# A hybrid decoder layer on one core: w_o split a head earlier and one tile per head, a new deal of the filling products, squares written to an operand block

## The chip, the core and the metric

The kernel runs on one core of one Trainium2 chip. The metric is the device time of one execution, in microseconds (us). Three runs of the kernel before gave 1396.53 to 1400.5 us, median 1399.54 us. Engine names in the profile: PE is TensorE (PEld its weight loads), DVE VectorE, ACT ScalarE, POOL GpSimd, SP the engine that issues the transfers.

## The reference

One decoder layer over 1024 tokens of width 1024, all in float32. Four retention heads and eight causal attention heads (latent attention, key width 96, value width 64) share one input projection; their outputs, 512 columns each, are joined and multiplied by one output matrix w_o. Two normalisations stand around the residual, then a SwiGLU with 2816 hidden columns and a gated embedding:

```python
def rmsnorm(x, w):
    xf = x.astype(jnp.float32)
    y = xf * lax.rsqrt(jnp.mean(xf * xf, axis=-1, keepdims=True) + EPS)
    return (y * w.astype(jnp.float32)).astype(x.dtype)
...
    return jnp.concatenate([ret_out, mla_out], axis=-1) @ w_o
...
        h = h + rmsnorm(mix, post_mix_norm[i])
        hn = rmsnorm(h, pre_ffn_norm[i])
        ff = (jax.nn.silu(hn @ w_gate[i]) * (hn @ w_up[i])) @ w_down[i]
        h = h + rmsnorm(ff, post_ffn_norm[i])
        e = rmsnorm(p[i] @ w_ple_proj[i], ple_norm[i])
        gate = jax.nn.sigmoid(h @ w_ple_gate[i] + b_ple_gate[i])
        h = h + e * gate
```

## The kernel before

Every float32 operand of a large product is split into a high and a low part: ACT casts the high part (line 81), DVE or POOL subtracts it for the low one (line 82). A product is then three matmuls, high by high, low by high and high by low (line 94). The splits of whole weight tiles are made by `slot` (line 102 issues the load of a tile `raw`, four buffers; the parts go into a ring of eight high/low slots, or into a place that is handed in as `hl`).

The order of each engine's own queue is set by a scheduler from the program's order, the waits and its own estimates of times; only the steady gate/up stage at the end has an order that is written out by hand. Buffers come from pools with a fixed count; PSUM has the tags s (two buffers of two banks), t, f and o.

The stages, with their places in the profiled execution:

- The input projection, the latent projections and the four retention heads, up to about 350 us. The retention outputs are stored to `md`.
- Sixteen products of p with w_pp, half of a row tile each, stored to `ed`; they run beside attention heads 0 and 1.
- The attention heads, `for h in range(NH)`, to about 564 us. Each head loads its k and q operands (`heads(h)`, lines 536 and 537, eight loads). For each of eight row blocks i there is a score product `sc` (PE, line 94), the masked minimum (DVE, line 612), the exponential (ACT, line 617), the reciprocal (DVE, line 620) and the scaling (POOL, line 621). Then pairs of blocks are transposed (`ptp`, PE, line 630), split into th and tl (ACT and DVE) and multiplied by the values (`po`, lines 641 and 642). Each half of a head ends with `os` (ACT and DVE, lines 647 and 648) and four stores to `mo` (line 650).
- Between them the filling products: the retention half of the output projection. `product_to` (lines 545 to 555) is a generator: each `advance` by one (line 557) makes one half row tile, 12 matmuls named `fill`, copied out by DVE (line 554) and stored to `od` once two are there. Sixteen are dealt: 2 after a head's first half and 1 after its second in heads 2 to 5, one after the first half in heads 6 and 7, the rest behind the last head (line 655). Their operands: `mr`, the four retention outputs (line 581; split into bh and bl, by ACT and POOL), and the first four tiles of w_o (`wo`, line 584, split by ACT and DVE), both at the head of `h == 2`. The other four tiles of w_o (`wo2`, line 652) are loaded and split at the end of head 4, into the upper halves of bh and bl.
- The output projection, `project(n)` for eight row tiles. It splits the attention output (`mh` by ACT, `ml` by POOL, two buffers each), multiplies it by wo2 into a PSUM tile `po3` of two banks (24 matmuls), and DVE adds the filling products' part out of PSUM into `mix` (line 715). ACT squares `mix` for the norm (line 717), POOL raises the mean to −1/2 (line 113), DVE scales (719) and adds the residual (720), SP stores (721), ACT squares again (723), DVE multiplies by the next norm's weights (725) and ACT scales (726). Both squares write their unused result into the same PSUM tile, so the tile is free for the next but one row tile only after line 723. `operands(n)` then transposes the rows into the operand blocks `xt` (PE, line 686, `ptx`; for the later four tiles POOL first makes the four subtractions of lines 739 to 742).
- The gate/up products `gu` (line 834) over the operand blocks, with weights loaded into `graw` and one of the `duo` tiles, summed by POOL, split, and used as `gh` and `gl`; the steady part, from 681 us, keeps PE busy without a gap. Then the down projection, the gate and the end.

The lines of the change: 584 and 587 (`wo`), 652 (`wo2`), 644 (the deal), 717 and 723 (the squares), 777 (`graw`) and 889 (`load(0)`).

Of the kernel before, what the change touches and what calls it, by code (L numbers as in the profile page):

```python
# [11 lines left out]
F32 = mybir.dt.float32  # L12
# [8 lines left out]
P = 128  # L21
# [41 lines left out]
def hybrid_layer(ctx: ExitStack, tc: tile.TileContext, a: dict, out: bass.AP):  # L63
# [508 lines left out]
    pe_ = scoped(st3, "pe", side="right")  # L572
    pm = scoped(st2, "pm", 2)
    vb = None

    for h in range(NH):
        kh_, kl_, qh, ql = heads(h) if h else first
        if h == 2:
            for k in range(RH):
                raw = raws.tile([P, S], F32, tag="raw", name=f"mr{k}")  # L580
                sp.dma_start(out=raw, in_=md[k])
                for c in range(2):
                    cs = slice(c * 512, (c + 1) * 512)
                    split(*bx(k, cs), raw[:, cs], sub=pool)
            wo = [slot(a["w_o"][k], name=f"o{k}") for k in range(4)]
            gen = product_to(od, [bx(k, slice(0, S)) for k in range(4)], wo, dve.tensor_copy)
            next(gen)
        if h == 1:
            vb = pm.tile([P, NT, 2 * VD], F32R, name="vb", bufs=1)
        vt = va if h % 2 == 0 else vb  # L590
        sp.dma_start(out=vt.bitcast(F32), in_=vd[h])
        for gg in range(2):
            cs = slice(gg * 512, (gg + 1) * 512)
            po = ps1("po", "of"[gg] if h >= 3 else "o")
            for g in (2 * gg, 2 * gg + 1):
                pb = []
                sc = ps2("sc") if g < 2 else None
                for i in (2 * g, 2 * g + 1):
                    n = (i + 1) * P
                    c1 = slice(i * P, (i + 1) * P)  # L600
                    if g >= 2:
                        sc = ps2("sc")
                    o = (i % 2) * 512 if g < 2 else 0
                    nc_ = 1 if n <= 512 else 2
                    w = max(n // nc_, 256)
                    for c in range(nc_):
                        products(sc[:, o + c * 512 : o + c * 512 + w],
                                 [(qh[:, c1], ql[:, c1], kh_[:, c * w : (c + 1) * w], kl_[:, c * w : (c + 1) * w])])
                    w = n // nc_
                    sv = sc[:, o : o + nc_ * 512].rearrange("p (c n) -> p c n", c=nc_)[:, :, :w]  # L610
                    nm = small.tile([P, 1], F32, name="nm")
                    dve.tensor_tensor_reduce(  # L612
                        out=sv, in0=sv, in1=cmask[:, S - n :].rearrange("p (c n) -> p c n", c=nc_),
                        scale=-1.0, scalar=3.0e38, op0=ALU.add, op1=ALU.min, accum_out=nm)
                    pr_ = pm.tile([P, S], F32, name="pr", bufs=5)
                    rs = small.tile([P, 1], F32, name="rs")
                    act.activation(pr_[:, :n].rearrange("p (c n) -> p c n", c=nc_), sv, AF.Exp, bias=nm, scale=-1.0,  # L617
                                   accum_out=rs)
                    ri = small.tile([P, 1], F32, name="ri")
                    dve.reciprocal(out=ri, in_=rs)  # L620
                    pool.tensor_tensor(out=pr_[:, :n], in0=pr_[:, :n], in1=ri.broadcast_to([P, n]), op=ALU.mult)  # L621
                    pb.append(pr_)
                last = 2 * g + 1
                for jj in range(g + 1):
                    blk = [(2 * jj, 0), (2 * jj, 1), (2 * jj + 1, 0), (2 * jj + 1, 1)]
                    if jj == g:
                        blk = [blk[0], blk[1], blk[3]]
                    pt = ps1("ptp")
                    for m, (kk, qq) in enumerate(blk):
                        pe.transpose(pt[:, m * P : (m + 1) * P], pb[qq][:, kk * P : (kk + 1) * P], ident)  # L630
                    nn = len(blk) * P
                    th = pm.tile([P, 512], F32R, name="th", bufs=4)[:, :nn]
                    tl = pm.tile([P, 512], F32R, name="tl", bufs=4)[:, :nn]
                    split(th, tl, pt[:, :nn])
                    off = (g % 2) * 256
                    for kk in (2 * jj, 2 * jj + 1):
                        if kk < last:
                            src, dst = slice((kk % 2) * 256, (kk % 2) * 256 + 256), slice(off, off + 256)
                        else:
                            src, dst = slice(256, 384), slice(off + 128, off + 256)  # L640
                        pe.matmul(po[:, dst], vt[:, kk, :], th[:, src], start=(kk == 0), stop=False)  # L641
                        pe.matmul(po[:, dst], vt[:, kk, :], tl[:, src], start=False, stop=(kk == last))  # L642
            if h >= 2:
                advance(gen, "fo"[gg], (2, 1)[gg] if h < 6 else 1 - gg)
            os_ = pm.tile([P, 512], F32, name="os")
            rows = slice((h % 2) * 64, (h % 2) * 64 + 64)
            act.copy(out=os_[rows], in_=po[64:])
            dve.tensor_tensor(out=os_[rows], in0=po[:64], in1=os_[rows], op=ALU.add)
            for i in range(4):
                sp.dma_start(out=mo[4 * gg + i][rows, h // 2, :], in_=os_[rows, i * P : (i + 1) * P])  # L650
        if h == 4:
            wo2 = [slot(a["w_o"][4 + k], name=f"o{4 + k}", hl=(bh[1][:, k, :], bl[1][:, k, :])) for k in range(4)]

    act.activation(small.tile([P, 1], F32, name="warm", bufs=1), rs, AF.Silu)
    advance(gen, "f", 2 * NT)
# [49 lines left out]
    def project(n):  # L705
# [6 lines left out]
        for c in range(2):  # L712
            cs = slice(c * 512, (c + 1) * 512)
            products(pt[:, cs], [(mh[:, k, :], ml[:, k, :], wo2[k][0][:, cs], wo2[k][1][:, cs]) for k in range(4)])
        dve.tensor_tensor(out=mix, in0=pt, in1=mix, op=ALU.add)
        ss = small.tile([P, 1], F32, name="s3")
        act.activation(pt, mix, AF.Square, accum_out=ss)
        rsqrt(ss, ss, 1.0 / D)
        dve.scalar_tensor_tensor(out=mix, in0=mix, scalar=ss, in1=wpm, op0=ALU.mult, op1=ALU.mult)
        dve.tensor_tensor(out=ht, in0=ht, in1=mix, op=ALU.add)  # L720
        sp.dma_start(out=hd[t], in_=ht)
        ss = small.tile([P, 1], F32, name="s3")
        act.activation(pt, ht, AF.Square, accum_out=ss)  # L723
        rsqrt(ss, ss, 1.0 / D)
        dve.tensor_tensor(out=mix, in0=ht, in1=wpf, op=ALU.mult)
        act.activation(mix, mix, AF.Copy, scale=ss)
# [29 lines left out]
    for n in range(NT):  # L756
        if n == 7:
            load_tiles(7)
        project(n)
        if n % 4 < 2:  # L760
            load_rows(n + (4 if n < 4 else 2))
        if n >= 2:
            operands(n - 2)
        if n < 4:
            load_tiles(n + 3)
    st_m.close()
    st_b.close()

# [5 lines left out]
    ghl = [[pg_.tile([P, 2, HALF], F32R, name=f"g{n}{i}") for n in "hl"] for i in (1, 2, 3, 0)]  # L774
    ghl = ghl[3:] + ghl[:3]
    quad = [v.rearrange("p (i n) -> p i n", i=4) for v in duo]
    graw = [pg_.tile([P, 4, HALF], F32, name="graw"), quad[0]]
    gga = [quad[2], quad[3]]
    gs = [v.rearrange("p (i n) -> p i n", i=3) for v in (strip[:, : 3 * HALF], strip[:, 3 * HALF :])] + [quad[4][:, :3]]
    wd = quad[4]  # L780
# [6 lines left out]
    def load(m):  # L787
        name, q = mats[m]
        sp.dma_start(out=graw[m % 2], in_=a[name][q])
# [96 lines left out]
    def when(i, f, *args):  # L886
        todo[i].append((f, args))

    load(0)
    load(1)  # L890
    weight_part(0, 0)
    weight_part(1, 0)
# [275 lines left out]
```

## Time and profile before

| | |
|---|---|
| median of three runs | 1399.54 us (1396.53 to 1400.5) |
| profiled execution | 1400.68 us |
| its span, first to last instruction | 1398.9 us |
| mean granted clock of TensorE | 0.986 |
| PE busy | 1336.5 us, 96% |
| DVE busy | 770.9 us, 55% |
| ACT busy | 541.8 us, 39% |
| POOL busy | 461.8 us, 33% |
| moved by transfers | 214.73 MB, 153 GB/s |

The span is taken from the first instruction to the last, so the execution's own time is a little longer (1.8 us here). Matmuls are pipelined, so a row of 0.39 us stands for a matmul that begins 0.23 us after the one before. In a row of the timeline, what stands in brackets is how long the engine was idle ahead of the row, and what ended that.

### The profile page before, as it was taken

Reading aid. Unit: us, or ns where it says so; the run is one execution under the profiler, and the core shown is the slowest. Engines: PE = TensorE matmul, PEld = TensorE weight load, DVE = VectorE, ACT = ScalarE, POOL = GpSimd, SP = SyncE. Lnnn points to the kernel's source line nnn. Section 1 sums busy time; section 2 is a strip of 40 time slices with the busy share of each in tenths; the row PEclk is TensorE's granted clock in tenths of the full one; section 3 lists DMA queues with packets and bytes.
Section 4 is the critical chain, followed back from the end, with each engine's and each line's share of the span. In section 5 each row is a group of like instructions: output and inputs, shape, how many; then the busy total and the mean of one; then the engine's idle time right before and its main releaser. Section 6 shows DMA issues by size and latency. Waiting matters only on the chain.

```text
span 1398.9 us, 18091 instructions
## 1 busy us (share of the span) xinstructions
PE 1336.5 (96%) x6756; PEld 1134.4 (81%) x6756; DVE 770.9 (55%) x1193; ACT 541.8 (39%) x898; POOL 461.8 (33%) x341
## 2 busy tenths in 40 slices
PE   7999999999989999887999999999999999999997
PEld 6987988988778887665788888888888788888886
DVE  6445637445566676488445444444445554474645
ACT  5443321011565555355343333333334444344521
POOL 1100000000363333248577666666664100012500
PEclk9999999999999999998999999999999999999999
DMA  7127831212474641743344344433346876565422
GB/s 251 46 92 250 265 118 39 75 23 60 143 232 123 200 131 30 273 135 123 121 165 149 146 173 173 169 138 144 140 178 218 269 234 211 178 218 193 138 102 75
DMA packets 85304, 214.73 MB, mean 153 GB/s; under 512 B 8992, under 2 KB 23840, under 8 KB 79584
## 3 DMA queue, kind: packets, MB, share of 16 engines
q1 hardware_dynamic: 85216, 213.58, 45.5%
q8 instruction: 53, 0.87, 0.3%
q14 instruction: 35, 0.29, 0.1%
HBM read 144.86 MB, written 67.63 MB: 152 GB/s over the span
## 4 chain that ended last, share of the span: by engine, by line
PE 83%; DMA 4%; DVE 4%; POOL 3%; issue 3%; ACT 2%; SPq 1%; DVEq 0%; ACTq 0%; POOLq 0%
PE gu L834 29%; PE db L1011 7%; PE pqk L94 6%; PE pg L94 6%; PE da L1011 6%; PE pa L94 4%; PE fill L94 3%; PE prv L94 3%; PE sc L94 3%; PE ptp L630 2%; PE prg L94 2%; PE pge L94 2%; PE po L642 1%; PE pq L94 1%; PE po L641 1%
## 5 line engine op out<-in xcount | busy, mean ns | idle before, releaser
L834 PE MATMUL gu<-x,gh 128*128 128x512 f32 x1232 | 383.6, 393 | 6.3 <-ACT po L723 5.6
L834 PEld LDWEIGHTS gu<-x,gh 128*128 128x128 f32 x1232 | 233.2, 190 | 55.7 <-ACT po L723 5.8
L834 PE MATMUL gu<-x,gl 128*128 128x512 f32 x616 | 241.2, 392 | 0.4 <-DVE gl L82 0.4
L834 PEld LDWEIGHTS gu<-x,gl 128*128 128x128 f32 x616 | 116.7, 189 | 25.1 <-DVE gl L82 0.7
L845 ACT COPY duo<-gu 128x512 f32<-128x512 f32 x66 | 38.9, 589 | 189.3 <-PE gu L834 189.3
L621 POOL TENSOR_TENSOR pr<-pr,ri 128x128 f32<-128x128 f32 (+3 forms) x64 | 74.8, 1178 | 105.7 <-DVE ri L620 98.4
L113 POOL TENSOR_TENSOR s<-s,mhalf 128x1 f32<-128x1 f32 x32 | 23.9, 752 | 238.4 <-DVE s L111 238.3
L113 POOL TENSOR_TENSOR gf<-gf,mhalf 128x4 f32<-128x4 f32 x8 | 8.1, 1008 | 266.7 <-DVE gf L111 266.7
L82 DVE TENSOR_TENSOR gl<-strip,gh 128x1024 fp32r<-128x1024 f32 (+1 forms) x44 | 61.6, 1399 | 33.3 <-ACT gh L81 33.3
L82 DVE TENSOR_TENSOR x<-draw,x 128x1024 fp32r<-128x1024 f32 (+1 forms) x43 | 48.1, 1135 | 46.9 <-ACT x L81 46.9
L82 DVE TENSOR_TENSOR gl<-graw,gh 128x1024 fp32r<-128x1024 f32 x22 | 33.8, 1538 | 72.5 <-ACT gh L81 72.5
L81 ACT CAST x<-draw 128x1024 fp32r<-128x1024 f32 (+1 forms) x47 | 45.2, 979 | 73.0 <-PE db L1011 20.6
L82 DVE TENSOR_TENSOR gl<-duo,gh 128x1024 fp32r<-128x1024 f32 x22 | 29.5, 1343 | 67.9 <-ACT gh L81 67.9
L850 DVE TENSOR_TENSOR duo<-gu,duo 128x512 f32<-128x512 f32 x66 | 45.4, 687 | 38.0 <-PE gu L834 37.9
L82 DVE TENSOR_TENSOR tl<-ptp,th 128x512 fp32r<-128x512 f32 (+1 forms) x80 | 49.8, 633 | 24.7 <-ACT th L81 23.7
L94 PE MATMUL pg<-x,x 128*128 128x512 f32 (+1 forms) x255 | 58.9, 378 | 0.0
L81 ACT CAST th<-ptp 128x512 fp32r<-128x512 f32 (+1 forms) x80 | 42.4, 544 | 41.9 <-PE ptp L630 41.6
L855 POOL TENSOR_TENSOR duo<-duo 128x512 f32<-128x512 f32 x11 | 23.3, 2122 | 103.2 <-DVE duo L818 103.2
L617 ACT ACTIVATE pr<-sc,nm 128x128 f32<-128x128 f32 (+3 forms) x64 | 47.7, 747 | 18.7 <-DVE nm L612 11.1
L94 PEld LDWEIGHTS pg<-x,x 128*128 128x128 f32 x255 | 45.8, 188 | 8.6
L612 DVE CUSTOM_DVE_ANT_0 sc<-sc,cmask 128x128 f32<-128x128 f32 (+3 forms) x64 | 48.0, 770 | 7.7 <-PE sc L94 7.3
L94 PE MATMUL pqk<-bl,hi_r 128*128 128x512 f32 x128 | 50.7, 396 | 0.0
(368 smaller groups left out, 3418.5 us busy)
## 6 DMA issues: line engine op xcount, KB each, us to landing
draw<-ld SPq DMA_DIRECT2D x58, 256.0 KB, 3.8
graw<-in_w_gate SPq DMA_DIRECT2D x11, 1024.0 KB, 8.6
duo<-in_w_up SPq DMA_DIRECT2D x11, 1024.0 KB, 4.7
duo<-in_w_down SPq DMA_DIRECT2D x11, 1024.0 KB, 5.1
td<-duo SPq DMA_DIRECT2D x11, 1024.0 KB, 4.4
ld<-duo SPq DMA_DIRECT2D x11, 1024.0 KB, 4.4
draw<-td SPq DMA_DIRECT2D x36, 256.0 KB, 4.1
ld<-duo SPq DMA_DIRECT2D x11, 768.0 KB, 6.7
```

Of the source, the lines that this page charges most:

```text
L81: act.copy(out=hi, in_=src)
L82: sub.tensor_tensor(out=lo, in0=src, in1=hi.bitcast(F32), op=ALU.subtract)
L94: pe.matmul(dst, l, r, start=(m == 0), stop=(m == n - 1))
L113: pool.tensor_tensor(out=dst, in0=dst, in1=mhalf[:, :n], op=ALU.pow)
L612: dve.tensor_tensor_reduce(out=sv, in0=sv, in1=cmask[:, S - n :].rearrange("p (c n) -> p c n", c=nc_), scale=-1.0, scalar=3.0e38, op0=ALU. ...
L617: act.activation(pr_[:, :n].rearrange("p (c n) -> p c n", c=nc_), sv, AF.Exp, bias=nm, scale=-1.0, accum_out=rs)
L621: pool.tensor_tensor(out=pr_[:, :n], in0=pr_[:, :n], in1=ri.broadcast_to([P, n]), op=ALU.mult)
L630: pe.transpose(pt[:, m * P : (m + 1) * P], pb[qq][:, kk * P : (kk + 1) * P], ident)
L834: pe.matmul(dst, l[:, at, ks], r[:, k, :], start=(n in (0, 1, 3) and x == 0), stop=(x == 11), skip_group_check=True)
L845: act.copy(out=s[nm], in_=dst)
L850: dve.tensor_tensor(out=s[nm], in0=dst, in1=s[nm], op=ALU.add)
L1011: pe.matmul(banks[j], l[:, ls], r[:, rs_], start=(fresh and q == 0 and m == 0), stop=(q == NQ - 1 and m == 2), skip_group_check=True)
```

## The change

- `wo` is made in the block of `h == 1` instead of `h == 2`: its four loads and splits come a head earlier in the program and take four of the eight ring slots there.
- `wo2` is made one tile at a time, at the end of heads 3, 4, 5 and 6, instead of four at the end of head 4.
- The filling products follow a table `FILL`, by head from 2 to 7 and half, and three are made inside the last head, ahead of its last products with the values.
- Both squares of `project` write into `junk`, a quarter of one operand block in SBUF (T4, of which that quarter is written only by the last row tile), seen as eight blocks of 128 columns, instead of into PSUM.
- The first load of w_gate is issued before the pools of the output projection are closed, into `duo[0]`; `graw` and `duo[0]` change places for w_gate and w_up in the whole steady stage.

```diff
+    wo2 = []
+
+    FILL = (0, 1), (2, 1), (1, 1), (1, 1), (1, 1), (0, 0)
...
-            wo = [slot(a["w_o"][k], name=f"o{k}") for k in range(4)]
             gen = product_to(od, [bx(k, slice(0, S)) for k in range(4)], wo, dve.tensor_copy)
             next(gen)
         if h == 1:
+            wo = [slot(a["w_o"][k], name=f"o{k}") for k in range(4)]
...
                     off = (g % 2) * 256
+                    if h == NH - 1 and g == 3 and jj < 3:
+                        advance(gen, "o", 1)
...
             if h >= 2:
-                advance(gen, "fo"[gg], (2, 1)[gg] if h < 6 else 1 - gg)
+                advance(gen, "fo"[gg], FILL[h - 2][gg])
...
-        if h == 4:
-            wo2 = [slot(a["w_o"][4 + k], name=f"o{4 + k}", hl=(bh[1][:, k, :], bl[1][:, k, :])) for k in range(4)]
+        if 2 < h < 7:
+            k = h - 3
+            wo2.append(slot(a["w_o"][4 + k], name=f"o{4 + k}", hl=(bh[1][:, k, :], bl[1][:, k, :])))
...
+        junk = xt[6][:, :, :, 3 * P :].rearrange("p h k n -> p (h k) n")
         ss = small.tile([P, 1], F32, name="s3")
-        act.activation(pt, mix, AF.Square, accum_out=ss)
+        act.activation(junk, mix.rearrange("p (b n) -> p b n", b=8), AF.Square, accum_out=ss)
...
-        act.activation(pt, ht, AF.Square, accum_out=ss)
+        act.activation(junk, ht.rearrange("p (b n) -> p b n", b=8), AF.Square, accum_out=ss)
...
+    sp.dma_start(out=duo[0].rearrange("p (i n) -> p i n", i=4), in_=a["w_gate"][0])
     st_m.close()
...
-    graw = [pg_.tile([P, 4, HALF], F32, name="graw"), quad[0]]
+    graw = [quad[0], pg_.tile([P, 4, HALF], F32, name="graw")]
...
-    load(0)
     load(1)
```

What this does to the engines' orders is seen in three places. First SP, in the loads and stores of heads 1 and 2. The order before, from the third `ed` store ahead of the retention loads on:

```order
L555 DMA ed_100<-fill 128x1024
L581 DMA mr_3859<-md 128x1024
L581 DMA mr_3865<-md 128x1024
L581 DMA mr_3871<-md 128x1024
L591 DMA va<-vd 128x1024
L650 DMA mo_114<-os 64x128
...
L555 DMA ed_101<-fill 128x1024
L581 DMA mr_3877<-md 128x1024
L102 DMA raw_o_3883<-in_w_o 128x1024
L102 DMA raw_o_3889<-in_w_o 128x1024
L650 DMA mo_110<-os 64x128
```

The changed order at the same place:

```order
L555 DMA ed_100<-fill 128x1024
L102 DMA raw_o_3597<-in_w_o 128x1024
L102 DMA raw_o_3603<-in_w_o 128x1024
L102 DMA raw_o_3609<-in_w_o 128x1024
L594 DMA va<-vd 128x1024
...
L102 DMA raw_o_3615<-in_w_o 128x1024
L555 DMA ed_101<-fill 128x1024
L584 DMA mr_3883<-md 128x1024
L536 DMA hi_k_3871<-kd_76 64x1024
L537 DMA hi_k_3871<-krd_82 32x1024
...
L537 DMA lo_q_3878<-qrd_81 32x1024
L584 DMA mr_3889<-md 128x1024
```

The w_o tiles stand where three retention loads stood. Head 2's k and q loads, which before stood in the rows ahead of all of this, now come behind them, and three retention loads last of all.

Second ACT, at the start of the output projection (`mh` is the high part of the attention output; `s` the sum of a square). Before:

```order
L81 CAST mh<-strip 128x512 x2
L717 ACTIVATE po_5763,s_5789<-duo_5741 128x1024
L81 CAST mh<-duo_5740 128x512
L723 ACTIVATE po_5763,s_5796<-duo_5742 128x1024
L717 ACTIVATE po_5809,s_5835<-duo_5738 128x1024
L81 CAST mh<-duo_5740 128x512
L726 ACTIVATE duo_5741<-duo_5741,s_5796 128x1024
```

Changed:

```order
L81 CAST mh<-strip 128x512 x2
L81 CAST mh<-duo_5740 128x512 x2
L81 CAST mh<-strip 128x512
L724 ACTIVATE x_5734,s_5789<-duo_5741 128x8x128
L81 CAST mh<-strip 128x512
L730 ACTIVATE x_5734,s_5796<-duo_5742 128x8x128
L724 ACTIVATE x_5734,s_5835<-duo_5738 128x8x128
L733 ACTIVATE duo_5741<-duo_5741,s_5796 128x1024
```

The squares write the operand block `x` instead of `po`, and the first of them stands behind five `mh` casts instead of two.

Third SP, at the first weight loads of the gate/up stage. Before:

```order
L721 DMA hd_91<-duo_5742 128x1024
L789 DMA graw<-in_w_gate 128x2048
L702 DMA duo_5741<-od_109 128x1024
L789 DMA duo_5738<-in_w_up 128x2048
L721 DMA hd_93<-duo_5742 128x1024
```

Changed:

```order
L797 DMA graw<-in_w_up 128x2048
L728 DMA hd_92<-duo_5742 128x1024
...
L728 DMA hd_91<-duo_5742 128x1024
L773 DMA duo_5738<-in_w_gate 128x2048
L728 DMA hd_93<-duo_5742 128x1024
```

w_up comes first now, four row tiles' stores earlier; w_gate stands behind the seventh row tile's store as before, but it writes a `duo` block that the transposes of an earlier row tile must have left.

## Rows read from the trace of the kernel before

**Rows 1.** The page's part 4: the chain that ended last, share of the span by engine.

```profile
PE 83%; DMA 4%; DVE 4%; POOL 3%; issue 3%; ACT 2%; SPq 1%; DVEq 0%; ACTq 0%; POOLq 0%
```

**Rows 2.** Stretches: length, busy PE, PEld, DVE, ACT, POOL (instructions), PEclk, DMA, GB/s.

```profile
399.80:428.90 29.10, 24.32 (x134) 20.23 (x134) 22.16 (x44) 20.22 (x41) 22.05 (x18) 0.94 0.73 207
428.90:450.40 21.50, 21.17 (x138) 19.09 (x137) 13.84 (x34) 10.91 (x26) 6.78 (x7) 1.00 0.48 119
...
472.60:499.60 27.00, 23.86 (x148) 21.16 (x146) 19.74 (x45) 15.96 (x32) 9.96 (x8) 1.00 0.64 189
499.60:526.50 26.90, 26.60 (x161) 23.81 (x162) 17.95 (x44) 14.23 (x32) 10.98 (x10) 1.00 0.46 135
...
546.40:571.90 25.50, 21.03 (x93) 16.74 (x92) 8.73 (x14) 8.66 (x15) 3.75 (x3) 0.80 0.23 70
571.90:680.60 108.70, 85.33 (x377) 67.46 (x376) 76.81 (x82) 51.53 (x82) 63.26 (x51) 0.89 0.48 170
...
655.90:662.70 6.80, 4.47 (x11) 3.51 (x12) 6.72 (x7) 3.20 (x5) 6.76 (x4) 0.50 0.19 77
...
681.00:1080.00 399.00, 399.00 (x1762) 330.41 (x1761) 189.32 (x192) 136.85 (x195) 251.24 (x162) 1.00 0.45 164
...
659.14:680.60 21.46, 18.01 (x67) 13.61 (x67) 10.28 (x11) 7.49 (x11) 15.91 (x12) 0.76 0.14 49
...
571.90:591.70 19.80, 17.59 (x81) 14.19 (x79) 11.31 (x12) 6.38 (x10) 6.38 (x7) 1.00 1.01 379
```

**Rows 3.** Timeline of PE, end of head 1 and head 2: waits.

```profile
403.31 0.38 PE L642 MATMUL po<-tl,vb 128*128 128x256 f32 x1 [0.36 <-DVE tl L82]
...
414.82 0.50 PE L94 MATMUL fill<-lo_o,bh 128*128 128x512 f32 x1 [1.34 <-DVE lo_o L82]
```

**Rows 4.** Timeline of PE, stretch from 472.6 us: its two longest waits.

```profile
493.11 0.38 PE L642 MATMUL po<-tl,va 128*128 128x256 f32 x1 [1.75 <-DVE tl L82]
498.00 0.55 PE L630 MATMUL ptp<-pack,pr 128*128 128x128 f32 x3 [0.98 <-POOL pr L621]
```

**Rows 5.** Who waited for instructions on po, 571.9 to 681 us (us, times).

```profile
  PE po L94: 9.2, 6
...
  PE gu L834: 5.6, 1
```

**Rows 6.** Timeline of SP's queue, the retention loads.

```profile
392.57 4.50 SPq L581 DMA_DIRECT2D mr<-md  x3
```

**Rows 7.** Timeline of POOL: retention splits; first subtraction of the last row tile.

```profile
404.25 5.00 POOL L82 TENSOR_TENSOR bl<-mr,bh 128x512 fp32r<-128x512 f32 x4
...
665.99 1.76 POOL L739 TENSOR_TENSOR duo<-duo 128x512 f32<-128x512 f32 x1 [0.44 <-ACT duo L726]
```

**Rows 8.** The chain of waits in order of time: start, us, what.

```profile
425.87 2.74 PE fill L94 x12
...
491.09 3.26 DMA raw_o<-in_w_o
...
565.41 1.90 DMA mo<-os
```

**Rows 9.** Timeline of DVE: a fill copy, an addition alone and beside POOL.

```profile
572.11 0.69 DVE L554 COPY fill<-fill 128x512 f32<-128x512 f32 x1 [3.09 <-PE fill L94]
...
582.64 1.22 DVE L720 TENSOR_TENSOR duo<-duo,duo 128x1024 f32<-128x1024 f32 x1
...
588.70 2.20 DVE L720 TENSOR_TENSOR duo<-duo,duo 128x1024 f32<-128x1024 f32 x1
```

**Rows 10.** Timeline of ACT: the first square, a cast, an activation into SBUF.

```profile
579.32 1.03 ACT L717 ACTIVATE po<-duo 128x1024 f32<-128x1024 f32 x1 [7.80 <-DVE duo L715]
...
582.91 0.62 ACT L81 CAST mh<-duo 128x512 fp32r<-128x512 f32 x1 [2.45 <-DMA duo<-mo]
...
664.76 1.15 ACT L726 ACTIVATE duo<-duo,s 128x1024 f32<-128x1024 f32 x1
```

**Rows 11.** The page's part 6: w_gate's loads, KB each, us to landing.

```profile
graw<-in_w_gate SPq DMA_DIRECT2D x11, 1024.0 KB, 8.6
```

## The prediction

> **What bounds the kernel now.** I began with the chain of waits that ended last: TensorE holds 83% of it, every other engine or transfer 4% or less [rows 1]. So the time goes down only where TensorE idles, runs at its lower clock, or issues less. I then cut the part that the change touches into stretches [rows 2], each from one head's last score product to the next head's. The steady gate/up stage from 681 us has PE busy for 399.0 of 399.0 us and the change leaves its work alone, so whatever moves its start moves the end by as much: the predicted difference is the shift of that start, now 680.6 us. The loss ahead of it lies in three places. Beside heads 1 and 2 PE is busy 24.3 of 29.1 us; in the last head 21.0 of 25.5 us at a mean clock of 0.80; in the output projection 85.3 of 108.7 us at 0.89. Last I read what ended PE's idle time: splits of w_o in the first place [rows 3] and in the stretch from 472.6 us [rows 4], the second square in the output projection [rows 5].
>
> **The change, part by part**
>
> *A. The w_o splits a head earlier, stretch 399.8 to 428.9 us.* Now PE waits 1.34 us for lo_o, and four times for tl behind the same splits on DVE, 0.36 us the first time [rows 3]. In the changed order w_o's splits fall in 398 to 408 us, where the mr loads stood, and the mr splits move behind, to 407 to 426 us. What is queued behind: on SP, seven of head 2's eight k/q loads now stand behind the raw_o loads and one of mr, and the eighth behind four stores of head 1; three mr loads, waiting for buffers, took 4.50 us to issue [rows 6]. Head 2's operands land near 414 us, where they were there long before. On POOL four bl splits take 5.00 us [rows 7], and head 2's normalisations queue behind them. Replaying the two orders with these durations I get the next boundary 0.5 us later: the lo_o wait goes and a wait for head 2's operands comes. Bounds: all these waits go (−3), or head 2 waits one more issue block of 4.50 us (+5).
>
> *B. 428.9 to 546.4 us, five stretches, 117.5 us.* By the order these hold 8 filling products where 12 stood (2, 2, 3, 4, 1 before; 0, 2, 3, 1, 2 now; the stretch ahead keeps 2). One is 12 matmuls and 2.74 us [rows 8], so 4 × 2.74 = 11.0 us of PE work go. Late next is the softmax chain on VectorE: the first stretch has 13.84 us of DVE work with two fill copies, of 0.69 us each [rows 2, 9], beside 21.5 us of span. So a stretch without fills still takes about 19.0 us (I take 2.5 of the 5.5 us that its two fills cost). The second is unchanged at 22.2. The third keeps its three fills and loses what a w_o tile does there, a wait of 1.75 us for tl and 0.98 for pr [rows 4] behind a load of which 3.26 us stand in the chain [rows 8]: 27.0 becomes 24.6. The fourth loses three fills, 8.2 us, of which I take 6.4: 20.5. The fifth gains one, and 19.9 becomes 22.2. Together 108.5 us, −9.0. Bounds: only the waits go (−3), or all the fill time and 2 us of waits do (−13).
>
> *C. Last head, 546.4 to 571.9 us.* Three fills go between head 7's transposes, three stand at the end instead of two. PE idles 4.5 us here at clock 0.80 [rows 2], so three fills, 8.2 us of work, find 4.5 us of idle time and a part of the half-clock time: +1.6 us, between −2 (they also keep the clock up) and +4 (8.2 less the idle time). Those at the end are covered by head 7's last stores and the load back, which hold the output projection until 571.9 us (the last store alone has 1.90 us in the chain [rows 8]); without that cover each would cost its 2.74 us.
>
> *D. Output projection, 571.9 to 680.6 us.* The squares no longer write the PSUM bank, so the next tile's products wait for the DVE addition instead of the second square. That wait is 9.2 us of PE in six and 5.6 us in one ahead of the first gate/up product [rows 5], 14.8 us in all, with half-clock stretches behind (6.8 us at 0.50 [rows 2]). But the order shows what takes its place. ACT now casts five mh ahead of the first square, where it cast two. There are two mh buffers, so the fifth waits until PE has finished tile 2: 571.9 + 72 × 0.228 + 2.74 + 0.62 = 591.7 us (0.228 is 2.74/12, 0.62 the cast), against 579.3 us [rows 10]. The first square is 12.4 us later, and all norms behind it. DVE is what must catch up: of its 76.8 us in this stage 10.3 lie behind the last norm step, at 659.1 us, and 0.7 is a fill copy [rows 2, 9]; three additions of 1.22 us, 3.7, come ahead of the square. That leaves 62.1 us, so the last norm step ends at 653.8 us if DVE never idles. Now it idles 67.4 − 55.2 = 12.2 us between 591.7 and 659.1 (its 76.8 less 11.3 and 10.3 [rows 2]); if it keeps all of that, the step ends at 666.0. The replay, row by row, gives 659.7 to 664.3; I take 662.1: +3. The tail behind it (normalise, four POOL subtractions of which the first takes 1.76 us [rows 7], transposes, splits) stays as long, so the steady stage starts 3 us later though PE itself waits less. w_gate's load, 1 MB and 8.6 us [rows 11], now waits for the operands of the sixth tile, whose block it takes; the first gate/up product waits for it although w_up's 24 stand behind. Issued near 650 us, it is landed and split near 662, beside the last norm step, and adds nothing unless that slips. Bounds of D: −9 and +12 (the rivals).
>
> *The squares themselves.* Sixteen ACT operations write SBUF instead of PSUM: 1.03 us into PSUM, 1.15 for an SBUF-to-SBUF activation of the same size [rows 10], so at most 16 × 0.12 = 1.9 us of ACT, hidden, since ACT is busy 51.5 of 108.7 us [rows 2]. The Trainium skill, "ScalarE: Activation LUTs", section "Step-by-step: what each stage is for", speaks against this edit: PSUM is ScalarE's faster destination, which helps only if TensorE doesn't need most of PSUM. By the bare rule the sum would be up to 1.9 us worse; its caveat holds here.
>
> *The rest.* The swap of the raw weight tiles renames buffers and gives the steady stage the same work: 0, from −1 to +1.
>
> **Sum.** 0.5 − 9.0 + 1.6 + 3.0 = −3.9 us. The profiled execution took 1400.68 us, so 1396.8; the median of the runs, 1399.54, is 1.1 lower, so I forecast **1396 us**, 0.25% less. About 0.3% (4.2 us) is what a measurement of this kernel can tell from no change.
>
> **The rivals**
>
> *R1, slower: the late first square isn't caught up.* DVE keeps its 12.2 us of idle time (+6.9), and five more of its norm passes run beside POOL: the same addition takes 1.22 us alone and 2.20 beside POOL's ml split [rows 9], so +5. D is +12 and the time 1399.5 − 6.9 + 12 = 1405 us. It decides once D exceeds the 6.9 us of A to C. For it: each norm is a chain over ACT, DVE and POOL. Against it: tiles overlap, and many passes are slow already. The Trainium skill, "GPSIMD Engine Reference", section "8. Key points", has GpSimd share its SBUF interfaces with VectorE, in contention when there are two SBUF inputs; the pair of durations agrees.
>
> *R2, much faster: the freed banks pay.* DVE never idles (653.8, −5.3), and half of one half-clock stretch of 6.8 us goes too (−3.4): D is −9, the time 1399.5 − 6.9 − 9 = 1384 us. Against it: nothing in a norm's chain is quicker than before.
>
> *R3, no change: the heads don't get shorter.* If the softmax chain sets each head's length, the fills removed were filling idle time and B is −3: 0.5 − 3 + 1.6 + 3 = +2, so 1402 us. For it: from 472.6 to 499.6 PE idles 3.1 us in spite of three fills. Against it: in B's first and fourth stretch PE is busy all but 0.3 us [rows 2].
>
> That the change doesn't do what it says is a small matter: the table deals none to head 2's first half, yet the order still puts two products ahead of its last scores; B counts by the order.
>
> **How the numbers follow.** Forecast 0.45, R1 0.20, R2 0.17, R3 0.18. The forecast lies at the 0.3% bound (1395.3 us): half of it counts as faster, half as same. R2 is faster, R3 same (0.145) or slower (0.035), R1 slower (0.175) or same. Faster 0.40, same 0.39, slower 0.21. The range, 1384 to 1408 us, takes in R1 with 3 us to spare, R3, and the slower half of R2.
>
> **What would show it.** Right: no PE wait on the second square, the first square near 20 us behind the stage's first product, the five stretches near 108 us, the steady stage from about 677 us. Wrong: the five stretches still over 114 us (R3); a steady start beyond 685 us with most DVE additions at 2.2 us (R1) or before 668 us (R2); head 2's first scores waiting over 5 us for hi_q or lo_q.

## The result and the profile after

The changed kernel took 1410.10 us (median of four runs, 1406.58 to 1410.98) against 1399.38 us: a ratio of 1.0080, interval 1.0058 to 1.0102. Repeated later beside other kernels it took 1412.72 us against 1396.83, ratio 1.0109 (1.0086 to 1.0132). It is slower by about 1%, and above the end of the range at 1408 us. In one run of those below, no_squares, one execution of twelve fell out (1512.24 us at a granted clock of 0.84); its time and ratio are those of the other eleven.

The stretches of the changed kernel, cut at the same events as [rows 2] (length; busy PE, PEld, DVE, ACT, POOL with instructions; granted clock; DMA share; GB/s):

```profile
399.50:431.30 31.80, 24.85 (x134) 20.40 (x134) 20.81 (x42) 20.61 (x42) 20.55 (x17) 0.89 0.87 244
...
450.20:475.50 25.30, 22.07 (x143) 19.67 (x142) 17.57 (x41) 13.91 (x30) 9.12 (x8) 1.00 0.55 161
475.50:501.90 26.40, 24.25 (x151) 21.49 (x150) 18.13 (x45) 15.38 (x33) 11.14 (x10) 1.00 0.50 145
...
542.90:570.70 27.80, 24.83 (x130) 20.41 (x129) 11.71 (x22) 9.76 (x18) 5.84 (x4) 0.94 0.22 63
570.70:685.20 114.50, 88.99 (x389) 70.75 (x389) 75.66 (x83) 52.02 (x83) 63.08 (x50) 0.81 0.47 167
...
590.50:661.80 71.30, 48.47 (x213) 38.40 (x212) 59.38 (x67) 40.74 (x67) 40.48 (x34) 0.72 0.43 144
```

The stretch of heads 1 and 2 (A) takes 31.8 us (29.1 before), the five stretches of B 111.6 (117.5), the last head (C) 27.8 (25.5), the output projection (D) 114.5 (108.7). The steady stage starts at 685.2 us instead of 680.6, and what lies behind that start takes 719.6 us instead of 718.3. This profiled execution, 1406.58 us, was the shortest of its four; that of before, 1400.68 us, was longer than each of the four timed beside it.

The wait that the squares were to remove is gone: where [rows 5] had 9.2 and 5.6 us behind the second square, nothing waits for it, and the gate/up products have 0.7 us of idle time left, for another reason (page, part 5):

```profile
L842 PE MATMUL gu<-x,gh 128*128 128x512 f32 x1232 | 382.3, 392 | 0.7 <-ACT x L81 0.7
```

What came in its place is the prediction's late first square. ACT's timeline at the start of the output projection:

```profile
582.13 0.62 ACT L81 CAST mh<-duo 128x512 fp32r<-128x512 f32 x1 [9.22 <-DMA duo<-mo]
...
589.99 0.62 ACT L81 CAST mh<-strip 128x512 fp32r<-128x512 f32 x1 [3.99 <-PE po L94]
590.52 1.06 ACT L724 ACTIVATE x<-duo 128x1024 fp32r<-128x1024 f32 x1
```

In this stage three casts stand ahead of the square, two that wait for transfers (9.22 and 2.62 us) and a third that waits 3.99 us for PE; the square starts 19.8 us behind the stage's first product, where it started 7.4 us behind. PE, no longer held by the banks, finishes its products early and then has nothing but transposes to wait for (timeline of PE, its longest waits there):

```profile
624.12 1.97 PE L692 MATMUL ptx<-pack,duo 128*128 128x128 f32 x8 [4.10 <-ACT duo L733]
633.90 1.11 PE L692 MATMUL ptx<-pack,duo 128*128 128x128 f32 x4 [7.82 <-ACT duo L733]
```

The stretch around them, columns as above:

```profile
622.00:663.00 41.00, 20.14 (x73) 14.83 (x74) 34.67 (x38) 23.74 (x38) 31.41 (x22) 0.50 0.41 142
```

Its granted clock is 0.50 for 41 us, that is 1.2 GHz instead of 2.4. So the waits for the square did not turn into time: they were exchanged for waits for the norms.

### The profile page after: what moved, and what is told of

The parts are those of the page before. It is cut to its first block, busy times and chain, and to the rows that moved or that the text cites. A ratio compares the mean times of both kernels' runs of the same rounds, so it can differ in the third digit from the quotient of the medians.

```text
span 1404.8 us, 18079 instructions
## 1 busy us (share of the span) xinstructions
PE 1335.7 (95%) x6756; PEld 1134.3 (81%) x6756; DVE 769.5 (55%) x1193; ACT 543.0 (39%) x898; POOL 460.1 (33%) x341
## 4 chain that ended last, share of the span: by engine, by line
PE 84%; DMA 3%; POOL 3%; issue 3%; DVE 3%; ACT 2%; SPq 1%; DVEq 0%; ACTq 0%; POOLq 0%
PE gu L842 29%; PE db L1018 8%; PE pqk L94 6%; PE pg L94 6%; PE da L1018 6%; PE pa L94 4%; PE prv L94 3%; PE fill L94 3%; PE po L94 3%; PE sc L94 3%; PE prg L94 2%; PE pge L94 2%; PE ptp L633 1%; PE pq L94 1%; PE po L647 1%
## 5 line engine op out<-in xcount | busy, mean ns | idle before, releaser
L81 ACT CAST x<-draw 128x1024 fp32r<-128x1024 f32 (+1 forms) x47 | 45.3, 980 | 71.5 <-PE da L1018 20.5
L82 DVE TENSOR_TENSOR gl<-duo,gh 128x1024 fp32r<-128x1024 f32 x22 | 33.7, 1533 | 70.2 <-ACT gh L81 70.2
L82 DVE TENSOR_TENSOR gl<-graw,gh 128x1024 fp32r<-128x1024 f32 x22 | 30.5, 1386 | 67.9 <-ACT gh L81 67.9
```

The lines of the kernel that those rows point to most:

```text
L81: act.copy(out=hi, in_=src)
L82: sub.tensor_tensor(out=lo, in0=src, in1=hi.bitcast(F32), op=ALU.subtract)
```

## The experiments

Lengths in us of the stages A to D in each run's profiled execution, by the same events; "square" is the first square's start behind the stage's first product; ratios are against the kernel before, timed beside each.

| run | ratio (95% interval) | A | B | C | D | square |
|---|---|---|---|---|---|---|
| before | 1 | 29.1 | 117.5 | 25.5 | 108.7 | 7.4 |
| the change | 1.0080 (1.0058 to 1.0102) | 31.8 | 111.6 | 27.8 | 114.5 | 19.8 |
| whole_again | 1.0109 (1.0086 to 1.0132) | 32.3 | 118.7 | 27.4 | 115.5 | 20.6 |
| squares_only | 1.0011 (0.9994 to 1.0029) | 28.8 | 117.9 | 23.6 | 106.2 | 10.3 |
| heads_only | 1.0023 (1.0008 to 1.0037) | 32.9 | 113.1 | 28.1 | 106.9 | 9.7 |
| gate_only | 0.9993 (0.9978 to 1.0008) | 26.6 | 117.9 | 22.6 | 106.7 | 8.0 |
| no_squares | 1.0030 (1.0011 to 1.0048) | 32.8 | 113.2 | 28.1 | 106.1 | 9.7 |
| four_in_tail | 1.0012 (0.9995 to 1.0030) | 32.0 | 116.1 | 28.9 | 105.1 | 11.9 |
| wo_back | 1.0047 (1.0029 to 1.0064) | 29.9 | 110.3 | 27.2 | 115.6 | 20.6 |
| wo_back_four_in_tail | 0.9972 (0.9952 to 0.9992) | 29.7 | 110.9 | 28.9 | 103.8 | 11.8 |
| old_deal | 1.0072 (1.0044 to 1.0099) | 33.5 | 122.1 | 27.0 | 107.1 | 13.8 |
| three_at_end | 0.9966 (0.9949 to 0.9983) | 31.9 | 114.8 | 22.6 | 105.4 | 9.8 |
| squares_three_at_end | 1.0027 (1.0013 to 1.0042) | 26.0 | 115.1 | 22.7 | 116.6 | 19.6 |
| wo_only | 0.9987 (0.9973 to 1.0002) | 34.5 | 119.3 | 22.7 | 102.6 | 7.4 |
| wo_first_in_two | 0.9979 (0.9961 to 0.9996) | 26.6 | 113.5 | 28.9 | 105.8 | 12.1 |
| wo2_only | 1.0031 (1.0013 to 1.0049) | 30.0 | 123.0 | 22.5 | 107.2 | 8.0 |
| fill_only | 0.9984 (0.9971 to 0.9997) | 28.0 | 111.7 | 28.1 | 106.3 | 9.7 |

**1. Three parts alone, and the change without its squares.** Theory S was that the squares cost, by pulling casts ahead on ACT; theory G that w_gate's later load does; theory H that the heads do.

squares_only, on the kernel before:

```diff
-        act.activation(pt, mix, AF.Square, accum_out=ss)
+        act.activation(junk, mix.rearrange("p (b n) -> p b n", b=8), AF.Square, accum_out=ss)
...
-        act.activation(pt, ht, AF.Square, accum_out=ss)
+        act.activation(junk, ht.rearrange("p (b n) -> p b n", b=8), AF.Square, accum_out=ss)
```

> The kernel before with nothing but both squares moved into the operand block. The order of ACT in the output projection then has one mh cast (of the third row tile) between the first addition and the first square, where the whole change has three. Theory S (the squares are what costs: once PE no longer waits for them, mh casts come ahead of the first square on ACT, the norms start late, PE runs out of work behind the products and falls to its lower clock): 3 to 8 us slower than before, 1402 to 1407 us, the output projection 112 to 116 us instead of 108.7. Theory G (the squares pay as such, what costs is w_gate's load behind an operand block): faster by 3 to 9 us, 1390 to 1396 us, no wait of PE on the second square.

Neither: 1397.77 us against 1397.18, no difference that can be told. Both theories fall in this form.

heads_only is the sum of wo_only, wo2_only and fill_only, whose diffs stand below:

> The kernel before with the three edits on the heads alone: w_o a head earlier, one tile of w_o per head, the new deal of the fills. Theory S: the heads behave as in the whole change (the output projection starts 1 us earlier) and the output projection as before, so 1397 to 1400 us, no change that a measurement can tell. Theory H (the edits on the heads lose more than their profile shows, by the clock of the stage behind them): slower by 3 us or more, 1402 us and above.

1400.10 us, 0.2% slower: at the upper end of S's band (1397 to 1400), under H's 1402, and unlike S had it, a difference that can just be told.

gate_only, on the kernel before:

```diff
+    sp.dma_start(out=duo[0].rearrange("p (i n) -> p i n", i=4), in_=a["w_gate"][0])
     st_m.close()
...
-    graw = [pg_.tile([P, 4, HALF], F32, name="graw"), quad[0]]
+    graw = [quad[0], pg_.tile([P, 4, HALF], F32, name="graw")]
...
-    load(0)
```

> The kernel before with nothing but the first w_gate load moved and the two raw weight tiles exchanged. Theory S: within 2 us of before, 1398 to 1402 us. Theory G: 4 to 6 us slower, 1403 to 1406 us, because the first gate/up product waits for w_gate's splits and the steady stage starts at 684 to 687 us.

1396.44 us, no difference. Theory G falls.

no_squares, on the changed kernel (the second square likewise):

```diff
-        act.activation(junk, mix.rearrange("p (b n) -> p b n", b=8), AF.Square, accum_out=ss)
+        act.activation(pt, mix, AF.Square, accum_out=ss)
```

> The changed kernel with both squares put back into PSUM, all else as changed. Theory S: the loss is gone, 1397 to 1401 us, against 1410 with the squares. Theory G: still 1404 us or more.

1400.38 us, 0.3% slower than before instead of 0.8 to 1.1%: the squares cost here, and alone they cost nothing that can be told. What costs must be the squares together with an edit on the heads.

**2. Which edit on the heads.** ACT's order tells what to try: squares alone leave one cast between the first addition and the first square, squares with three fills at the end put three there.

four_in_tail, on the changed kernel, alters one number, so that two fills stand at the end again:

```diff
-                    if h == NH - 1 and g == 3 and jj < 3:
+                    if h == NH - 1 and g == 3 and jj < 4:
```

> The changed kernel with one number altered: four fills instead of three inside the last head, so two instead of three stand at its end. In ACT's order one mh cast instead of three then comes between the first addition and the first square. Theory S2 (neither the squares nor the deal costs alone; the third fill at the end, together with the freed banks, puts the mh casts ahead of the first square): the first square comes near 583 us instead of 590.5, the output projection takes 105 to 109 us instead of 114.5, the time 1398 to 1403 us against 1410. Rival L (PE idles in the middle of the stage and falls to its lower clock whatever the place of the first square, because the products are done early): the stage stays above 112 us and the time at 1407 us or more.

1399.68 us, S2's band. ACT's timeline:

```profile
587.93 0.62 ACT L81 CAST mh<-duo 128x512 fp32r<-128x512 f32 x1 [10.69 <-DMA duo<-mo]
588.45 1.05 ACT L724 ACTIVATE x<-duo 128x1024 fp32r<-128x1024 f32 x1
```

One cast, no wait for PE, the square 11.9 us behind the first product and the stage 9.4 us shorter than in the change. The square's absolute time was missed (588.5, not 583): the heads ended 6 us later in this execution. Rival L falls: PE's mean clock in the stage is only 0.85 (0.81 in the change), and yet the stage takes 105.1 us.

wo_back, on the changed kernel:

```diff
+            wo = [slot(a["w_o"][k], name=f"o{k}") for k in range(4)]
             gen = product_to(od, [bx(k, slice(0, S)) for k in range(4)], wo, dve.tensor_copy)
             next(gen)
         if h == 1:
-            wo = [slot(a["w_o"][k], name=f"o{k}") for k in range(4)]
```

> The changed kernel with w_o back in the block of head 2. ACT's order in the output projection keeps three mh casts ahead of the first square. Theory S2: the stretch of heads 1 and 2 falls from 31.8 to 28 to 30 us, because head 2's k and q operands are loaded ahead of w_o again; the output projection stays at 112 to 116 us; the time is 1405 to 1408 us. Rival H (the move of w_o is what costs, in every stage behind it too): 1399 us or less.

1403.91 us, a little under S2's band; its stages as S2 expected, 29.9 and 115.6 us.

wo_back_four_in_tail has both diffs:

> Both alterations together. Theory S2: the heads' gain stays and both losses go, 1393 to 1398 us, at or below the kernel before. Rival L: above 1402 us, the output projection above 112 us.

1393.31 us, within S2's band and 0.28% under the kernel before. Ratios of the two alterations multiply: from 1.0080, the one takes it to 1.0012, the other to 1.0047, both to 0.9972.

old_deal, on the changed kernel:

```diff
-                    if h == NH - 1 and g == 3 and jj < 3:
-                        advance(gen, "o", 1)
...
-                advance(gen, "fo"[gg], FILL[h - 2][gg])
+                advance(gen, "fo"[gg], (2, 1)[gg] if h < 6 else 1 - gg)
```

> The changed kernel with the old deal of the fills (2 and 1 in heads 2 to 5, 1 and 0 in heads 6 and 7, two at the end). ACT's order has two mh casts between the first addition and the first square. Theory S2: between the two orders, the output projection 107 to 113 us, the time 1400 to 1407 us. Theory F (the new deal costs by itself): 1400 us or less.

1408.47 us, over S2's band, and theory F falls. Its output projection is 107.1 us, as S2 expected for two casts, but B took 122.1 us and A 33.5: the early w_o and the w_o tiles one per head are paid there, with no fills taken out. Its last head also drew a low clock (27.0 us at 0.68).

**3. The pair alone, on the kernel before.** three_at_end takes one fill out of the last head, so three stand at the end:

```diff
-                advance(gen, "fo"[gg], (2, 1)[gg] if h < 6 else 1 - gg)
+                advance(gen, "fo"[gg], (2, 1)[gg] if h < 6 else (1 - gg) * (7 - h))
```

> The kernel before with one filling product fewer in the last head, so three stand at the end as in the change; squares in PSUM. ACT's order has the first square ahead of the third mh cast. Theory S2: the output projection stays at 106 to 109 us, the time within 3 us of the kernel before. Rival E (the third fill at the end costs by itself, by holding up the first tile's products): 4 us or more slower.

1392.47 us, 0.34% faster, more than S2 had, and rival E falls. It has the lowest ratio of the study, though wo_back_four_in_tail's interval overlaps with its own. The fill that left B now stands between the halves of the first tile's products, and D takes 105.4 us, no more than elsewhere.

squares_three_at_end adds the two lines of squares_only:

> The kernel before with the squares in the operand block and three fills at the end, nothing else of the change. Squares alone gave +0.1%. The order of ACT now has three mh casts ahead of the first square, as in the whole change. Theory S2 (it is this order, and not the heads, that costs): first square near 20 us behind the stage's first product, the output projection 113 to 117 us, 5 to 9 us slower than before, 1403 to 1407 us. Rival (the loss needs the edits on the heads): within 3 us of before.

1401.34 us, 0.27% or 3.1 us slower than before, just beyond the rival's 3 us and under S2's band (1403 to 1407), which had left out what the third fill at the end gives; square and stage came as S2 said. Against three_at_end it is 0.6% slower, so the squares cost 0.1% with two fills at the end and 0.6% with three. First three_at_end, timeline of ACT:

```profile
579.01 1.03 ACT L717 ACTIVATE po<-duo 128x1024 f32<-128x1024 f32 x1 [7.80 <-DVE duo L715]
```

Then squares_three_at_end:

```profile
582.37 0.62 ACT L81 CAST mh<-strip 128x512 fp32r<-128x512 f32 x1 [3.52 <-PE po L94]
582.90 1.06 ACT L718 ACTIVATE x<-duo 128x1024 fp32r<-128x1024 f32 x1
```

The square stands behind the cast that waits for PE, and D is 11.2 us longer (116.6 against 105.4), beside heads that keep their old order of w_o. By the medians the two kernels are 8.9 us apart; in the profiled pair A differs too, by 5.9 us the other way, without an edit there.

wo_only, on the kernel before:

```diff
-            wo = [slot(a["w_o"][k], name=f"o{k}") for k in range(4)]
             gen = product_to(od, [bx(k, slice(0, S)) for k in range(4)], wo, dve.tensor_copy)
             next(gen)
         if h == 1:
+            wo = [slot(a["w_o"][k], name=f"o{k}") for k in range(4)]
```

> The kernel before with w_o moved to the block of head 1 and nothing else. Theory A (head 2's k and q operands, loaded behind w_o, land near 416 us and hold up its first scores): the stretch of heads 1 and 2 takes 31 to 33 us instead of 29, PE waits there for lo_q or lo_k, 2 to 5 us slower than before in all. Rival: the splits of w_o are only moved, 0 plus or minus 1.5 us.

The stretch is as long as theory A said and more (34.5 us), but not for its reason: PE waits 0.29 us there for lo_q, and 2.26 and 1.91 us for tl and bh, at a mean clock of 0.80. Nor is the kernel slower: 1395.78 us, and its output projection, at 102.6 us, is the shortest of all. Why the later stages give the 5 us back here is not settled.

wo_first_in_two, on four_in_tail:

```diff
         if h == 2:
+            wo = [slot(a["w_o"][k], name=f"o{k}") for k in range(4)]
             for k in range(RH):
...
-            wo = [slot(a["w_o"][k], name=f"o{k}") for k in range(4)]
```

> The change with four fills in the last head and w_o made at the head of head 2's block, ahead of the retention loads but behind head 2's own k and q loads. The splits of w_o fall beside head 1 as in the change; only the k and q loads are early again. Theory A: the stretch of heads 1 and 2 falls to 27 to 30 us and the time to 1391 to 1395 us, as with w_o back behind the retention loads or better. Rival W (the splits beside head 1 are what costs there): the stretch stays above 31 us, the time at 1396 to 1400 us.

1394.64 us, inside theory A's band, and 26.6 us for the stretch, though with one fill in it instead of two; with 2.74 us for that it would be 29.3. Its PE still waits 2.46 us for tl, behind the w_o splits on DVE, and 1.91 us for bh, so theory A's time came without its reason being shown.

**4. The heads' other edits alone**, each on the kernel before. wo2_only:

```diff
-        if h == 4:
-            wo2 = [slot(a["w_o"][4 + k], name=f"o{4 + k}", hl=(bh[1][:, k, :], bl[1][:, k, :])) for k in range(4)]
+        if 2 < h < 7:
+            k = h - 3
+            wo2.append(slot(a["w_o"][4 + k], name=f"o{4 + k}", hl=(bh[1][:, k, :], bl[1][:, k, :])))
```

> The kernel before with one tile of w_o's second half at the end of heads 3 to 6 each, and nothing else. The prediction's step (the waits behind w_o in the stretch from 472.6 us go): 1 to 3 us faster. Theory B2 (each tile's cast stands in ACT's queue ahead of exponentials and waits for its own load, in two heads instead of one): 0 to 4 us slower, with PE waits of 2 to 3 us on the exponential in two stretches.

1401.06 us, 0.3% slower: the prediction's step is refuted and theory B2 holds in the main. ACT and PE between the last scores of heads 3 and 4 (timeline; `pr` is what the exponential writes):

```profile
461.12 1.04 ACT L81 CAST bh<-raw_o 128x1024 fp32r<-128x1024 f32 x1 [1.98 <-DMA raw_o<-in_w_o]
...
462.81 0.45 PE L94 MATMUL sc<-hi_k,hi_q 96*128 96x320 f32 x1 [2.16 <-ACT pr L618]
```

The stretch before and here, columns as above:

```profile
450.40:472.60 22.20, 21.84 (x142) 19.65 (x141) 16.47 (x40) 12.82 (x29) 9.12 (x8) 1.00 0.57 163
...
451.00:477.10 26.10, 23.59 (x142) 20.91 (x141) 17.50 (x41) 13.87 (x30) 9.11 (x8) 0.93 0.54 152
```

The cast of the w_o tile waits for its load, the exponentials stand behind it, and PE behind those; the stretch takes 26.1 us instead of 22.2. The next stretch, the one that the prediction's step names, did get shorter, 25.0 us against 27.0, but the fourth and fifth took 28.1 and 22.3 against 26.9 and 19.9, so B is 5.5 us longer. The wait at head 5's scores is 1.30 us, shorter than B2 said.

fill_only:

```diff
+    FILL = (0, 1), (2, 1), (1, 1), (1, 1), (1, 1), (0, 0)
...
+                    if h == NH - 1 and g == 3 and jj < 3:
+                        advance(gen, "o", 1)
...
-                advance(gen, "fo"[gg], (2, 1)[gg] if h < 6 else 1 - gg)
+                advance(gen, "fo"[gg], FILL[h - 2][gg])
```

> The kernel before with the new deal of the fills alone, three of them inside the last head and three at the end, squares in PSUM. The prediction's terms B and C without the w_o waits: heads 2 to 6 shorter by 6 to 9 us, the last stretch 2 us longer, 4 to 8 us faster in all. Rival R3 (the heads don't get shorter by fewer fills): within 2 us of before.

1394.74 us, 0.16% or 2.1 us faster, just beyond R3's 2 us and short of the 4 to 8 us that B and C promised. B does get shorter, by 5.8 us, but the last head takes 28.1 us where six runs without fills between its transposes take 22.5 to 23.6, at clocks of 0.92 to 1.00 (before and old_deal, at 0.80 and 0.68, took 25.5 and 27.0).

whole_again is the changed kernel itself:

> The changed kernel as it is, once more. All theories: 1406 to 1411 us; first square 19 to 21 us behind the first product of the output projection, that stage 112 to 117 us.

1412.72 us (1407.89 to 1416.18), over the band of 1411 at the median; square and stage inside theirs. The first wait behind a w_o tile, in PE's timeline:

```profile
463.98 0.63 PE L94 MATMUL sc<-hi_k,hi_q 96*128 96x320 f32 x1 [3.32 <-ACT pr L620]
```

The two stretches with such waits, columns as above:

```profile
451.00:479.70 28.70, 25.03 (x144) 22.03 (x142) 17.60 (x41) 13.93 (x30) 9.11 (x8) 0.88 0.49 143
479.70:509.90 30.20, 27.25 (x151) 24.32 (x149) 18.36 (x45) 15.23 (x33) 11.14 (x10) 0.89 0.47 125
```

In the first profile of the change these two took 25.3 and 26.4 us at clock 1.00. Here the clock fell to its lower level behind each wait (0.50 from 464 to 470 us and from 495 to 501, with PE busy throughout), and with it the two stretches are 7.2 us longer. That is more than all that B had gained (118.7 us, against 117.5 before).

## Why the prediction was wrong

By the two profiles the change took 5.9 us more, where the sum said 3.9 less. Of the 9.8 us between them B has 3.1, D 2.8, A 2.2 and C 0.7; 1.3 lie behind the start of the steady stage, and A began 0.3 us earlier. In whole_again B alone is 10.2 us over its term.

**B failed at "The second is unchanged at 22.2" and at "the third … loses what a w_o tile does there".** The first put the w_o tile that now stands at the end of head 3 at nothing; the second took away the old wait and put no new one in its place. One tile per head doesn't remove the wait; it repeats it. The load as the chain of waits of the changed kernel has it:

```profile
454.36 6.69 DMA raw_o<-in_w_o
```

Then ACT and PE (timeline):

```profile
461.07 1.04 ACT L81 CAST bh<-raw_o 128x1024 fp32r<-128x1024 f32 x1 [2.70 <-DMA raw_o<-in_w_o]
...
462.75 0.41 PE L94 MATMUL sc<-hi_k,hi_q 96*128 96x320 f32 x1 [2.88 <-ACT pr L620]
```

The load is issued behind four stores and three loads of the next head, and PE waits 2.88 us; in the third stretch it waits 1.75 us for `pr`, behind the next tile's cast. The five stretches were forecast at 19.0, 22.2, 24.6, 20.5 and 22.2 us and took 18.9, 25.3, 26.4, 19.4 and 21.6: the ones without such a wait were right within 1.1 us, the two with it 1.8 to 3.1 us short, and in whole_again 6.5 and 5.6. B was −5.9 in one execution and +1.2 in the other.

**D's term, +3, was too small; its choice of 662.1 us came out.** The late square came as worked out, 19.8 us behind the first product. The choice puts the end of the last norm step 90.2 us behind the stage's start, and it ended there after 91.1 (at 661.8 us). Two errors cancelled in that, which is luck: DVE idled 11.9 of the 71.3 us from the square to the last norm step, where the choice allowed 8.3 and the kernel before had 12.2, but had 59.4 us of work there and not 62.1. What failed is "The tail behind it … stays as long": it took 23.4 us instead of 21.5. In it the last norm's power on POOL, behind the sums of the weight parts, starts 8.1 us behind the last norm step, where it started 4.6 us behind. POOL's timeline before, then in the changed kernel:

```profile
663.74 0.54 POOL L113 TENSOR_TENSOR s<-s,mhalf 128x1 f32<-128x1 f32 x1
...
669.85 1.55 POOL L113 TENSOR_TENSOR s<-s,mhalf 128x1 f32<-128x1 f32 x1
```

The seven profiles with both the squares in the operand block and the exchange of the weight tiles have tails of 23 to 27 us, the other ten 19.6 to 21.5; what makes it so is open.

The profile of before also hid a part of the price. With the order that puts three casts first the stage takes 114.5 to 116.6 us in four profiles, with any other order 102.6 to 108.7 in thirteen: before's 108.7 was the long end of its own kind, and by the means the order costs nearer 10 us. In the pair three_at_end and squares_three_at_end the square is 9.8 us later and the last norm step 10.3, so nothing is caught up there. That is the first half of rival R1, at 0.20. Its second half (norm passes slowed beside POOL) did not occur: the residual additions had a median of 1.69 us, against 2.17 before. Nor did its sum come true, which has A to C at −6.9 us and D at +12: they measured −0.9 and +5.8. And the late square needs two edits: the prediction did not see that the squares with two fills at the end cost nothing that can be told.

**A and C were mis-sized.** A: +0.5 was forecast, +2.7 measured. Across the runs the stretch takes 31.8 to 34.5 us with w_o early (seven runs) and 26.0 to 31.9 without (nine, leaving out wo_first_in_two). The wait foreseen for head 2's operands is there, but small (PE 0.7 us on lo_q); PE waits longer for tl behind the w_o splits (2.26 us) and for bh (1.92 us), and at a lower clock. C: +1.6 was forecast and +2.3 came out of the two profiles, but before's last head had itself drawn a low clock (0.80); against the 22.5 to 23.6 us of six other runs three fills there (27.2 to 28.1 us in six profiles) cost about 5 us, over the bound of +4.

**What was right**: no wait on the second square, the order of ACT and the time of the first square, the price of the squares on ACT (1.06 us against 1.03, so 0.5 us in sixteen), and, by gate_only, nothing from the exchange of the weight tiles and from w_gate's place alone. B's terms for the fills, −6.6 us together, were near the −5.8 of fill_only.

Multiplied, the parts alone give 0.9987 × 1.0031 × 0.9984 × 0.9993 = 0.9995 for w_o, the w_o tiles, the deal and w_gate, and 1.0061 for the squares with three fills at the end: 1.0056. The change measured 1.0080 and 1.0109. The rest fits w_o's move, which costs nothing alone but 0.3 to 0.4% inside the change (wo_back, and four_in_tail against wo_back_four_in_tail); how it interacts is open.

## What to carry to other kernels

When a buffer is freed so that one engine can run ahead, read what the engines behind it will now find first in their queues: an operation that waits for the engine running ahead can come to stand in front of the one that starts the long chain. Work that waits for a load doesn't get cheaper when it is dealt out one piece per stage, as long as each load is issued just ahead of that piece; issuing each a stage earlier was not tried here. And a stage's length is taken from several executions before differences of a few microseconds are added up: here one profile of before stood 2 to 3 us high in two stages.

## What the runs showed that I had not expected

A wait of PE of 2 to 3 us can have two prices. In the change's two profiles the first wait behind a w_o tile was 2.88 us and 3.32 us; behind the first the stretch ran at clock 1.00 and took 25.3 us, behind the second at 0.88 and took 28.7. It is not the length of the wait alone: in wo2_only PE ran at the lower clock behind a wait of 2.16 us. Of the 9.6 us between the change's two profiled executions 7.2 lie in these two stretches. And taking one filling product out of the last head and doing it among the first products of the output projection, with no other edit, gave 0.34%, more than any part of the change gave alone.
